# Norms by column sums, true transposes, paired doubling steps and an alternating chain in a PE-bound hybrid decoder step

## The chip, the cores and the metric

One core of a Trainium2 chip runs the whole program. The metric is the device time of one execution in microseconds, as the median of several runs; lower is better. The profile is of one further execution.

## The reference

The program is one inference step of a one-layer decoder with d_model 1024: a prompt of 512 tokens with 16 learned meta tokens in front (528), and 8 sample sequences of 4 tokens, 560 columns in all.

```python
h = rms_norm(x, g_mix); proj = h @ w_in          # all input projections at once
# branch A: GLU -> causal depthwise conv (width 31) -> LayerNorm -> swish -> w_cout
# branch B, 8 heads of 128:
qkv_c = silu(causal_depthwise_conv(qkv, qkv_buf, w_short))   # width 4
q = l2_normalize(heads(q)) * D_HEAD ** -0.5; k = l2_normalize(heads(k)); v = heads(v)
# per chunk (gdn_intra, gdn_inter):
A = tril(beta * (k @ k.T) * decay, -1) + I
value, kcum = solve(A, [v * beta, k * beta * exp(G)])
u = value - kcum @ S
o = q_dec @ S + (q @ k.T * decay) @ u
S = S * exp(g_last) + k_dec.T @ u
o = rms_norm(o, g_head) * silu(z); dn_out = o @ w_dout
mix = sigmoid(gate_c) * conv_out + sigmoid(gate_d) * dn_out
x = x + mix @ w_o
x = x + square(relu(rms_norm(x, g_mlp) @ w_up)) @ w_down      # final rms_norm follows
```

Every matmul has to be of fp32 quality. The states of convolutions and heads come in for the sample sequences and go out for all.

## The kernel before, in words

Activations lie transposed: channels on the 128 partitions, tokens along the free axis. A projection chunk (L605, `gemm`) is 128 output channels: for each of 8 blocks of input channels the weights are split into a high part `wh` and a rest `wl`, the input likewise, and three products are summed, each over two halves of the tokens. That is 48 matmuls of 272 to 280 columns for a chunk. The chunks go in a fixed order: k of all heads first, then GLU pairs mixed with q, v and z of head after head, the gates, then w_dout ("do"), which needs all heads, then the gate of branch A, w_cout, w_o and the MLP (L2054, L2196).

Everything else is threaded between these matmuls by a planner written in Python, the `Weaver`. Each piece of work is a generator that yields (engine, cost, what it depends on). The planner keeps one clock for each engine and at every turn emits the instruction that could start earliest; ties go by priority. The costs are guesses written in the code, as 0.22 for a matmul. Once emitted, each engine runs its own list strictly in order: what the planner misjudged becomes a wait. The planner adds 0.5 us between a result of ACT and a matmul that reads it.

The prompt's delta rule runs in 4 chunks ("quarters", j) of 128 tokens; the last 16 prompt tokens and the 32 sample tokens are a fifth piece of 48. The parts that the change touches:

- `doubling` (L1041): the inverse of the 128 x 128 triangular matrices of all 32 (head, quarter) pairs is built up by blocks. Its last step multiplies 64 x 64 blocks: 32 matmuls at L1100, their results copied to SBUF by ACT and DVE in four lots, 32 matmuls at L1111, four lots copied again.
- `head_prep` (L1380), one head after another: squares of q, v and k turned to token-major. It holds one PSUM bank `b4` for the short piece: `v4` and `k4` are turned by a matmul with the identity (L1403, L1405), k times q is formed (L1407), and the sums of squares of q come token-major from five matmuls that load the squares and stream one column of ones (L1411). Then v (L1444), k (L1453), the product k q (L1461) and its masking on DVE in four pieces (L1465); the first masked piece releases `chain`.
- `chain` (L1473): for each quarter, k S and q S (L1495, L1497), R on DVE (L1501) and a scaled copy on ACT (L1504), the solve (L1510), the copy u (L1512), and two products of u (L1514, L1517) for the new S and the output. All use one PSUM bank `bx`, whose four column ranges have fixed roles. Afterwards the sample sequences: eight products with their states in 32-column tiles (L1538), a zero fill (L1542), the prompt's tail rows (L1544), a copy on ACT (L1546), and two selection matmuls (L1549) that add the samples' rows to what L1542 and L1544 wrote.
- `head_post` (L1631): norm and gate of the head's output, turned back by L1652 and, for the short piece, by a matmul with 48 columns of the identity (L1661).

An fp32 matmul with full operands runs as two passes (x2 in the rows, each with its own weight load); a transpose and the split projection products run as one. `column_sums` (L864) is the form that the norms of x and k use already: ones (or one column of ones) of 32 columns are loaded, the squares are streamed, and the four blocks of tokens go to four groups of 32 output partitions. Its result is turned to token-major by `sums_to_tokens` (L872; L882 a transpose, L885 a small matmul).

## Time and profile before

| | us |
|---|---|
| runs before: median, lowest, highest (3) | 1068.65, 1068.43, 1073.45 |
| the profiled execution's own time | 1068.22 |
| its span | 1066.4 |
| PE busy | 1047.8 (98%) |
| DVE busy | 767.8 (72%) |
| ACT busy | 623.1 (58%) |
| POOL busy | 149.2 (14%) |

The span is the time from the first to the last instruction that the profile has. Busy time is the time in which at least one instruction of the engine was under way; matmuls overlap, so a busy PE can still lose time between them. In the chain of waits every piece begins where the one before ends, so its length is what the program waited for it. "x10" counts passes, not matmuls.

### The profile page before, as it was taken

How to read it: one execution, taken by the hardware profiler on the slowest of the kernel's cores; microseconds unless marked ns; L12 is line 12 of the kernel's file. 1: busy time of each engine (PE TensorE's matmuls, PEld its weight loads, DVE VectorE, ACT ScalarE, POOL GpSimd, SP SyncE). 2: the span in 40 equal slices, each digit the busy share in tenths (PEclk: the TensorE clock that was granted, in tenths of full speed). 3: DMA queues.
4: the chain of work that ended last, by engine and by line, in shares of the span. 5: the costliest groups of instructions: out<-in, count | busy, mean ns of one | idle time of the engine just before them, and what ended most of it. 6: DMA issues, size and time to landing. Idle time of an engine off the chain costs nothing.

```text
span 1066.4 us, 21825 instructions
## 1 busy us (share of the span) xinstructions
PE 1047.8 (98%) x8835; PEld 1025.5 (96%) x8835; DVE 767.8 (72%) x1354; ACT 623.1 (58%) x1285; POOL 149.2 (14%) x173
## 2 busy tenths in 40 slices
PE   8999999999999999999999999999999999999997
PEld 6989999999999999999999999989999999999996
DVE  5888879788889887789953456897458547745754
ACT  5577344668787878775359334677327426723741
POOL 2067211102211221122111000000000000000000
PEclk9999999999999999999999999999999999999999
DMA  6232677466676566678876422753365365346212
GB/s 213 82 90 74 131 173 159 102 141 154 147 174 158 146 141 160 148 178 193 174 168 159 165 98 80 184 143 104 100 183 129 100 159 136 102 118 169 80 61 84
DMA packets 57872, 145.55 MB, mean 136 GB/s; under 512 B 14612, under 2 KB 20140, under 8 KB 57772
## 3 DMA queue, kind: packets, MB, share of 16 engines
q1 hardware_dynamic: 46828, 104.32, 30.5%
q0 software_dynamic: 10944, 39.85, 23.1%
q8 instruction: 69, 1.13, 0.4%
q14 instruction: 31, 0.25, 0.1%
HBM read 135.14 MB, written 9.01 MB: 135 GB/s over the span
## 4 chain that ended last, share of the span: by engine, by line
PE 85%; DVE 7%; DMA 3%; ACT 2%; issue 2%; SPq 0%; POOL 0%; POOLq 0%; DVEq 0%; ACTq 0%
PE pg L605 42%; PE pg L2196 17%; PE bk L2054 15%; DMA pre<-in_sq_dram 1%; DVE V L1209 1%; DVE acc L807 1%; DVE of L807 1%; PE bk L1411 1%; PE bk L1510 1%; PE bk L1514 1%; PE bk L970 1%; PE bk L1517 1%; PE bk L1495 1%; DMA M<-in_xT_dram 1%; PE bk L1497 1%
## 5 line engine op out<-in xcount | busy, mean ns | idle before, releaser
L605 PE MATMUL pg<-R,wh 128*128 128x280 f32 (+2 forms) x1920 | 279.3, 294 | 1.0 <-ACT pre L795 1.0
L605 PEld LDWEIGHTS pg<-R,wh 128*128 128x128 f32 x1920 | 253.6, 189 | 3.9 <-issue 1.5
L1209 DVE SCALAR_TENSOR_TENSOR V<-V,vec,V 128x512 f32<-128x512 f32 x240 | 180.5, 780 | 2.2
L560 ACT ACTIVATE wh<-wraw 128x1024 fp32r<-128x1024 f32 (+1 forms) x89 | 93.4, 1049 | 94.2 <-PE pg L605 79.0
L605 PE MATMUL pg<-R,wl 128*128 128x280 f32 (+2 forms) x960 | 143.9, 294 | 0.0
L605 PEld LDWEIGHTS pg<-R,wl 128*128 128x128 f32 x960 | 128.5, 189 | 1.4 <-issue 1.0
L573 POOL DMA_DIRECT2D wl<-in_w_dram x60 | 52.6, 877 | 343.1 <-ACT wl L571 246.2
L2001 ACT ACTIVATE whm<-RT 128x512 fp32r<-128x512 f32 x73 | 45.6, 626 | 55.3 <-PE pg L2196 40.2
L571 ACT ACTIVATE wl<-wh 128x1024 fp32r<-128x1024 f32 x60 | 63.5, 1058 | 14.8 <-PE pg L605 12.9
L1956 POOL DMA_DIRECT2D RT<-in_wu_dram x16 | 13.9, 866 | 384.1 <-DVE wlm L2004 123.1
L2004 DVE TENSOR_TENSOR wlm<-RT,whm 128x512 fp32r<-128x512 f32 x73 | 50.0, 687 | 16.6 <-issue 8.4
L2054 PE MATMUL bk<-R,whm 128*128 128x272 f32 x340 | 58.3, 288 | 0.7 <-ACT Tt L2095 0.7
L2196 PE MATMUL pg<-RD,whm 128*128 128x272 f32 (+2 forms) x272 | 57.7, 288 | 0.0
L2196 PE MATMUL pg<-K,whm 128*128 128x272 f32 (+2 forms) x272 | 57.5, 288 | 0.0
L605 PE MATMUL pg<-K,wh 128*128 128x272 f32 x256 | 53.0, 288 | 0.2 <-DVE K L1758 0.2
L605 PE MATMUL pg<-RD,wh 128*128 128x272 f32 x256 | 53.1, 289 | 0.0
L2054 PEld LDWEIGHTS bk<-R,whm 128*128 128x128 f32 x340 | 48.7, 188 | 0.9 <-ACT Tt L2095 0.9
L2196 PE MATMUL pg<-RD,M 128*128 128x272 f32 x264 | 46.2, 288 | 0.0
L2054 PE MATMUL bk<-R,M 128*128 128x272 f32 x258 | 45.5, 288 | 0.0
L2001 ACT ACTIVATE whm<-wrawm 128x512 fp32r<-128x512 f32 x43 | 26.8, 623 | 31.6 <-PE pg L2196 29.7
L2212 DVE TENSOR_TENSOR V<-pg,pre 128x544 f32<-128x544 f32 x29 | 21.0, 724 | 32.1 <-PE pg L2196 32.1
L577 DVE TENSOR_TENSOR wl<-wraw,wh 128x1024 fp32r<-128x1024 f32 x28 | 35.1, 1252 | 12.1 <-ACT wh L560 8.0
(485 smaller groups left out, 2453.3 us busy)
## 6 DMA issues: line engine op xcount, KB each, us to landing
wraw<-in_w_dram SPq DMA_DIRECT2D x87, 512.0 KB, 3.6
wl<-in_w_dram POOLq DMA_DIRECT2D x60, 512.0 KB, 5.6
RT<-in_wu_dram SPq DMA_DIRECT2D x24, 512.0 KB, 4.9
RT<-in_wu_dram POOLq DMA_DIRECT2D x16, 512.0 KB, 6.5
wrawm<-in_wn_dram SPq DMA_DIRECT2D x16, 512.0 KB, 3.4
RT<-in_wn_dram SPq DMA_DIRECT2D x16, 512.0 KB, 3.5
M<-in_sd_dram SPq DMA_DIRECT2D x16, 256.0 KB, 3.6
out_osd_dram<-M SPq DMA_DIRECT2D x16, 256.0 KB, 4.0
```

The source lines that it names most:

```text
L560: nc.scalar.activation(wh[:, c[0]:c[1]], w[:, c[0]:c[1]], AF.Copy)
L571: nc.scalar.activation(wl, wh.bitcast(F32), AF.Copy, scale=-1.0)
L573: nc.gpsimd.dma_start(wl, i["w"][n].bitcast(F32R), accum_op=ALU.add)
L577: nc.vector.tensor_tensor(wl, w, wh.bitcast(F32), op=ALU.subtract)
L605: nc.tensor.matmul(pt[:, hf, 0:N], w[idx][:, k, :], x[:, off + hf * N:off + hf * N + N], start=k == 0 and not part and x is hi, stop=k == ...
L807: nc.vector.scalar_tensor_tensor(acc[:, 0:584], pr[:, q:q + 584], vcol(w + q), acc[:, 0:584], op0=ALU.mult, op1=ALU.add)
L1209: nc.vector.scalar_tensor_tensor(cc[:, 0:512], G[r][:, 16 + q:528 + q], vcol(w + q), cc[:, 0:512], op0=ALU.mult, op1=ALU.add)
L2001: nc.scalar.activation(hi, raw, AF.Copy)
L2004: nc.vector.tensor_tensor(lo, raw, hi.bitcast(F32), op=ALU.subtract)
L2054: nc.tensor.matmul(acc[an], w[:, kp, :], x, start=kp == 0 and not part and x is hi and m not in (3, 6, 7), stop=kp == 3 and part == 1, ski ...
L2196: nc.tensor.matmul(out, w[:, k % 4, :], x[:, a], start=n_ == 0 and x is hi, stop=n_ == len(STEPS) - 1)
L2212: nc.vector.tensor_tensor(halves(tmp[:, 0:NPOST]), pt[:, :, 0:NPH], halves(ml["r2"]), op=ALU.mult)
```

## The change

The diff, cut to its core:

```diff
@@ kfin
-            nc.vector.tensor_tensor(st["sk"][:], st["s"][:], st["ed"][:], op=ALU.mult)
@@ doubling
-            for m in range(32):
+            def first(m, cost):
+                tb_[m // 8] = yield op("pe", cost, tn[m // 16], tb)
                 nc.tensor.matmul(B[m // 8][64:128, m % 8, :], KT[0:64, m, 64:128], Tn[0:64, m, :], start=True, stop=True)
+            def second(m, cost):
+                q = m // 8
+                tb_[q] = yield op("pe", cost, t1[q], *tc_[2 * (m // 16):2 * (m // 16) + 2])
+                nc.tensor.matmul(B[q][0:64, m % 8, :], P2[m // 16][64:128, m % 16, :], CTT[64:128, m, 64:128],
                                  start=True, stop=True)
+            for q in (0, 1):
+                for m in range(8 * q, 8 * q + 8):
+                    yield from first(m, 0.116)
+                yield from keep(q)
+            for q in (2, 3):
+                for m in range(8 * q, 8 * q + 8):
+                    yield from first(m, 0.07)
+                    yield from second(m - 16, 0.07)
+                yield from keep(q)
+                yield from done(q - 2)
+            for q in (2, 3):
+                for m in range(8 * q, 8 * q + 8):
+                    yield from second(m, 0.116)
+                yield from done(q)
@@ head_prep
-            nc.tensor.matmul(b4[:96, 0:128], M2["v4"], ident, start=True, stop=True)
-            nc.tensor.matmul(b4[:wk, 128:256], k4, ident, start=True, stop=True)
-            nc.tensor.matmul(b4[:wk, 384:432], k4, kq4[:, hh, :, 1], start=True, stop=True)
-            for j in range(5):
-                w = 128 if j < 4 else 96
-                nc.tensor.matmul(b4[:w, 432 + j:433 + j], sq[:, 128 * j:128 * j + w], ones[:, 0:1], start=True, stop=True)
+            nc.tensor.transpose(b4[:96, 0:128], M2["v4"], ident)
+            if wk > 64:
+                nc.tensor.transpose(b4[:wk, 128:256], k4, ident)
+            else:
+                nc.tensor.matmul(b4[:wk, 128:256], k4, ident, start=True, stop=True)
+            nc.tensor.matmul(b4[:wk, 256:304], k4, kq4[:, hh, :, 1], start=True, stop=True)
+            ts = yield from column_sums(b4[:, 304:480], sq, ones[:, 0:32], t, tb4)
...
-                nc.scalar.activation(kx[r:r + 32], b4[:32, 128:256], AF.Copy, scale=st["sk"][:32, hh, 4:5])
+                nc.scalar.activation(kx[r:r + 32], b4[:32, 128:256], AF.Copy, scale=st["ed"][:32, hh, 4:5])
...
+            nc.scalar.activation(sq[:, 0:128], b4[:, 304:432], AF.Copy)
+            nc.scalar.activation(sq[96:128, 128:176], b4[96:128, 432:480], AF.Copy)
+            nc.tensor.transpose(b4[:, 304:432], sq[:, 0:128], ident)
+            nc.tensor.matmul(b4[0:48, 432:464], sq[96:128, 128:176], ident[96:128, 96:128], start=True, stop=True)
             if hh >= 2:
                 yield wait(("post", hh - 2))
+            nc.vector.tensor_scalar(ssq[:, 0:4], b4[:, 304:432:32], 1e-6, 128.0 * 128.0 * EPS, op0=ALU.add, op1=ALU.mult)
+            nc.vector.tensor_scalar(ssq[:48, 4:5], b4[:48, 432:433], 1e-6, 128.0 * 128.0 * EPS, op0=ALU.add, op1=ALU.mult)
...
-            for j in range(4):
-                nc.vector.scalar_tensor_tensor(at[:, j, :], b[:, 128 * j:128 * j + 128], st["s"][:, hh, j:j + 1],
-                                               Ds[hh][:, j, :], op0=ALU.mult, op1=ALU.mult)
+            nc.vector.tensor_tensor(at, b.rearrange("p (t c) -> p t c", c=128), Ds[hh], op=ALU.mult)
+            W.spawn(chain(hh), -1)
@@ chain
+                ba, bu = (bx[:, 256:384], bx[:, 0:128]) if j % 2 else (bx[:, 0:128], bx[:, 256:384])
-                    t = yield op("pe", 0.22, ts, to)
-                    nc.tensor.matmul(bx[:, 0:128], ks, S, start=True, stop=True)
+                    t = yield op("pe", 0.22, ts)
+                    nc.tensor.matmul(ba, ks, S, start=True, stop=True)
...
-                t = yield op("pe", 0.3, t, t2, tr, tbx)
-                nc.tensor.matmul(bx[:, 256:384], CT["T"][:, 4 * hh + j, :], rr, start=True, stop=True)
-                nc.scalar.activation(u, bx[:, 256:384], AF.Copy)
+                t = yield op("pe", 0.3, t, to, tr, tbx)
+                nc.tensor.matmul(bu, CT["T"][:, 4 * hh + j, :], rr, start=True, stop=True)
+                nc.scalar.activation(u, bu, AF.Copy, scale=st["s"][:, hh, j:j + 1])
...
-            for a in range(2):
-                nc.tensor.matmul(bx[64 * a:64 * a + 32, 256:384], zsel[:, 32:64], ident, start=True, stop=True)
-                nc.tensor.matmul(bx[64 * a + 32:64 * a + 48, 256:384], kq4[:, hh, 32:48, a], S, start=True, stop=True)
             for g in range(2):
                 nc.tensor.matmul(bx[0:96, 256:384], cst[:, C_SL + 96 * g:C_SL + 96 * g + 96], Wt[:, g, :],
-                                 start=False, stop=g == 1, skip_group_check=True)
+                                 start=g == 0, stop=False, skip_group_check=True)
+            for a in range(2):
+                nc.tensor.matmul(bx[64 * a + 32:64 * a + 48, 256:384], kq4[:, hh, 32:48, a], S, start=False,
+                                 stop=a == 1, skip_group_check=True)
...
-            nc.scalar.activation(u[:48], bx[:48, 0:128], AF.Copy)
+            nc.scalar.activation(u[:48], bx[:48, 0:128], AF.Copy, scale=st["s"][:48, hh, 4:5])
@@ head_post
-            nc.tensor.matmul(b4[:, 0:48], ob[:, 4, :], ident[:, 0:48], start=True, stop=True)
+            nc.tensor.transpose(b4[:, 0:128], ob[:, 4, :], ident)
```

In words. The squares of q are summed by `column_sums` into four groups of partitions, copied to SBUF by two ACT instructions, and turned to token-major by a transpose and a small matmul in the same bank; the two DVE instructions that finish the norm come after that, and so do the steps of v and k that follow in `head_prep`. The turns of `v4`, `k4` (but for the last head) and of the output's short piece become transposes. The factor s = beta / |k|^2 no longer scales kd, kx and the masked product but u, in its copy. The masked product is one DVE instruction over all four quarters. In `chain` the column ranges of the output product and of the solve swap from quarter to quarter, so that the first product of a quarter is written where u was read, not where the output is being read. The two zero fills go; the tail rows are added after the selection matmuls. In the last step of `doubling`, half of the two sets of matmuls are issued in turns. Two memsets and a product on DVE go.

## Rows read from the trace of the kernel before

**Rows 1.** The page, part 1: busy us, share of the span, instructions

```profile
PE 1047.8 (98%) x8835; PEld 1025.5 (96%) x8835; DVE 767.8 (72%) x1354; ACT 623.1 (58%) x1285; POOL 149.2 (14%) x173
```

**Rows 2.** Windows, 187 to 492 us: busy us (instructions) by engine, granted clock, DMA

```profile
187.00:492.00 305.00, 302.32 (x2604) 292.90 (x2604) 254.28 (x497) 235.91 (x626) 60.25 (x71) 1.00 0.65 151
```

**Rows 3.** Waits, PE's longest and one of ACT's: us in total, times, longest

```profile
PE bk L1495 <- ACT M L1529: 1.6, 2, 1.0
...
ACT M L1504 <- DVE M L1501: 9.4, 14, 1.3
```

**Rows 4.** Chain of waits from 25 us: start us, us, what (x passes)

```profile
25.36 18.77 PE pg L605 x144
```

**Rows 5.** Chain of waits, first head's preparation

```profile
202.93 2.04 PE pg L605 x16
204.98 0.22 PE bk L1403 x2
...
205.42 0.13 PE bk L1407 x2
205.55 1.02 PE bk L1411 x10
206.57 1.89 PE pg L605 x14
208.46 0.44 PE bk L1444 x4
```

**Rows 6.** Chain of waits, norm of k and its turning back

```profile
96.65 1.33 PE bk L869 x29
97.98 2.52 PE pg L605 x18
100.50 0.11 PE bk L882
100.61 0.20 PE bk L885 x2
100.81 1.24 PE pg L605 x8
```

**Rows 7.** Chain of waits, sample stage of two heads

```profile
403.54 0.36 PE bk L1538 x8
403.90 0.45 PE pg L605 x2
...
471.67 0.36 PE bk L1538 x8
...
472.24 2.97 PE pg L605 x22
475.21 0.44 PE bk L1549 x4
```

**Rows 8.** Chain of waits, doubling; then the line of its third 32x32 product

```profile
189.12 3.87 PE bk L1100 x64
192.99 1.75 PE pg L605 x12
194.74 3.87 PE bk L1111 x64
...
L1084 PE MATMUL bk<-RT,M x64: 191/191/212, 183.8 to 185.8; 32*32 32x32 f32 x64
```

**Rows 9.** Groups of ACT by line, 187 to 492 us: busy us, mean ns | idle

```profile
L571 ACT ACTIVATE wl<-wh 128x1024 fp32r<-128x1024 f32 x33 | 35.0, 1059 | 0.1
...
L1504 ACT ACTIVATE M<-bk,st_eG 128x128 f32<-128x128 f32 x24 | 8.8, 366 | 9.4 <-DVE M L1501 9.4
L1512 ACT ACTIVATE M<-bk 128x128 f32<-128x128 f32 x32 | 8.7, 271 | 4.8 <-PE bk L1510 4.6
```

**Rows 10.** Timeline at the end of the heads: DVE, then PE

```profile
488.94 0.71 DVE L1677 TENSOR_TENSOR K<-zs,RD 128x544 fp32r<-128x544 f32 x1
...
495.51 0.41 PE L605 MATMUL pg<-RD,wh 128*128 128x272 f32 x2
```

More of the change, by code (lines that the diff above doesn't have):

```diff
@@ L1314, in m2 @@
                 m2_["kd"] = [cut(640).rearrange("p (t c) -> p t c", c=128) for _ in range(2)]
-                aa = [cut(608) for _ in range(2)]
+                aa = [cut(560) for _ in range(2)]
                 m2_["aa"] = aa
@@ L1428, in head_prep @@
             tx = yield op("act", 0.25, t4)
-            nc.scalar.activation(kd[32:48, 4, :], b4[32:48, 128:256], AF.Copy, scale=st["sk"][32:48, hh, 4:5])
+            nc.scalar.activation(kd[32:48, 4, :], b4[32:48, 128:256], AF.Copy, scale=st["ed"][32:48, hh, 4:5])
             if hh >= 2:
@@ L1434, in head_prep @@
                 tx = yield op("act", 0.25, t4)
-                nc.scalar.activation(kx[r:r + 32], b4[:32, 128:256], AF.Copy, scale=st["sk"][:32, hh, 4:5])
-            t = yield op("dve", 0.2, tx)
-            nc.vector.scalar_tensor_tensor(kx[64:96], b4[:32, 128:256], st["sk"][:32, hh, 4:5], kx[0:32].bitcast(F32),
+                nc.scalar.activation(kx[r:r + 32], b4[:32, 128:256], AF.Copy, scale=st["ed"][:32, hh, 4:5])
+            tk = yield op("dve", 0.2, tx)
+            nc.vector.scalar_tensor_tensor(kx[64:96], b4[:32, 128:256], st["ed"][:32, hh, 4:5], kx[0:32].bitcast(F32),
                                            op0=ALU.mult, op1=ALU.subtract)
-            E(("kx", hh)).set(t)
-            put_bank(kb4, t)
+            E(("kx", hh)).set(tk)
+            yield op("act", act_c(128), ts)
+            nc.scalar.activation(sq[:, 0:128], b4[:, 304:432], AF.Copy)
+            t = yield op("act", act_c(48), ts)
+            nc.scalar.activation(sq[96:128, 128:176], b4[96:128, 432:480], AF.Copy)
+            yield op("pe", 0.12, t)
+            nc.tensor.transpose(b4[:, 304:432], sq[:, 0:128], ident)
+            t = yield op("pe", 0.06, t)
+            nc.tensor.matmul(b4[0:48, 432:464], sq[96:128, 128:176], ident[96:128, 96:128], start=True, stop=True)
+            if hh >= 2:
+                yield wait(("post", hh - 2))
+            t1 = yield op("dve", 0.1, t)
+            nc.vector.tensor_scalar(ssq[:, 0:4], b4[:, 304:432:32], 1e-6, 128.0 * 128.0 * EPS, op0=ALU.add, op1=ALU.mult)
+            t1 = yield op("dve", 0.1, t)
+            nc.vector.tensor_scalar(ssq[:48, 4:5], b4[:48, 432:433], 1e-6, 128.0 * 128.0 * EPS, op0=ALU.add, op1=ALU.mult)
+            E(("ssq", hh)).set(t1)
+            put_bank(kb4, max(t1, tk))
             b, kb, tb = yield from get_bank()
@@ L1455, in head_prep @@
                 tx = yield op("act", 0.25, t)
-                nc.scalar.activation(kd[:, j, :], b[:, 128 * j:128 * j + 128], AF.Copy, scale=st["sk"][:, hh, j:j + 1])
+                nc.scalar.activation(kd[:, j, :], b[:, 128 * j:128 * j + 128], AF.Copy, scale=st["ed"][:, hh, j:j + 1])
             put_bank(kb, tx)
@@ L1462, in head_prep @@
                                  q[:, 128 * j:128 * j + 128], start=True, stop=True)
-            for j in range(4):
-                t1 = yield op("dve", 0.263, t)
-                nc.vector.scalar_tensor_tensor(at[:, j, :], b[:, 128 * j:128 * j + 128], st["s"][:, hh, j:j + 1],
-                                               Ds[hh][:, j, :], op0=ALU.mult, op1=ALU.mult)
-                E(("at", hh, j)).set(t1)
-                if j == 0:
-                    E(("ready", hh)).set(max(t1, tx))
-                    W.spawn(chain(hh), -1)
+            t1 = yield op("dve", dve_c(512), t)
+            nc.vector.tensor_tensor(at, b.rearrange("p (t c) -> p t c", c=128), Ds[hh], op=ALU.mult)
+            E(("at", hh)).set(t1)
             put_bank(kb, t1)
+            E(("ready", hh)).set(max(t1, tx))
+            W.spawn(chain(hh), -1)
         def chain(hh):
@@ L1508, in chain @@
                     t, t2 = tr, 0.0
-                t = yield op("pe", 0.3, t, t2, tr, tbx)
-                nc.tensor.matmul(bx[:, 256:384], CT["T"][:, 4 * hh + j, :], rr, start=True, stop=True)
+                t = yield op("pe", 0.3, t, to, tr, tbx)
+                nc.tensor.matmul(bu, CT["T"][:, 4 * hh + j, :], rr, start=True, stop=True)
                 tu = yield op("act", 0.17, t)
-                nc.scalar.activation(u, bx[:, 256:384], AF.Copy)
+                nc.scalar.activation(u, bu, AF.Copy, scale=st["s"][:, hh, j:j + 1])
                 t = yield op("pe", 0.22, tu)
                 nc.tensor.matmul(bx[:, 384:512], kd[:, j, :], u, start=True, stop=True)
-                ta = yield wait(("at", hh, j))
+                ta = yield wait(("at", hh))
                 to = yield op("pe", 0.22, tu, ta)
-                nc.tensor.matmul(bx[:, 0:128], at[:, j, :], u, start=True, stop=True)
+                nc.tensor.matmul(ba, at[:, j, :], u, start=True, stop=True)
                 Sn = Sb[j % 2]
```

56 lines of the change are left out of this document (17 added, 39 removed).

## The prediction

> **What bounds the kernel now.** I read the page's busy times first. TensorE (PE) is busy for 98% of the span, so it decides unless another engine starves it [rows 1]. Next comes the stage in which the change works, read by windows: from the doubling to the last head's output, 187 to 492 us, PE is busy 302 of 305 us, VectorE (DVE) 254 and ScalarE (ACT) 236, and the granted clock is 1.00, the 2.4 GHz level [rows 2]. The waits come third: the longest entry for PE in the whole trace is 1.6 us [rows 3]. So in this stage the heads' small matmuls are threaded between those of the projections (L605), and an instruction taken from PE shortens the stage by what it took there, whatever it did to latency; time taken from DVE or ACT is worth nothing unless PE waits for it. The busy share can't price these instructions, since matmuls overlap in it. The chain of waits can: where it runs along PE, its pieces join end to end, and a piece is what PE needed to get past that work. There a projection matmul takes 0.130 us at 280 columns (18.77 / 144) and 0.1275 at 274 (2.04 / 16) [rows 4, 5].
>
> **Head preparation, before.** Row by row: v4 0.22, k4 likewise 0.22, kq 0.13, the five column-of-ones sums 1.02, and the 14 projection matmuls behind them take 1.89 where 14 x 0.1275 is 1.78, so 0.11 more: 1.70 us for a head [rows 5]. A transpose is one pass instead of two: four take 0.44, 0.11 each [rows 5].
>
> **Head preparation, after.** The new sums use a form that the trace has in the norm of k: 32 loaded columns, four such tiles side by side. Sixteen of them (32 passes, of which the chain names 29) take 1.33, and the 18 projection matmuls behind take 2.52 instead of 2.34, so 1.51 in all [rows 6]. That isn't four times the price of four. The sample stage shows why: eight passes of 32-column tiles take 0.36, and the two projection matmuls after them 0.45 instead of the 0.255 of two at 274 columns, 0.56 in all; the next eight passes without a projection between take only 0.57 - 0.36 = 0.21 (472.24 - 471.67 is 0.57) [rows 7]. So going from whole-width matmuls into tiles and back costs 0.35 each time, and the work itself little. Four sums alone are then (1.51 - 0.35) / 4 + 0.35 = 0.64. Turning them back is the pair L882 and L885: 0.11 + 0.20, and eight projection matmuls at 1.24 instead of 1.04, 0.51 [rows 6]; it stands apart from the sums, because two ACT copies come between. After: v4 and k4 0.11 each, kq 0.13, sums 0.64, turning back 0.51, together 1.50, or 0.20 less for a head. Eight heads give -1.5, since the last one keeps its k4 matmul.
>
> The Trainium skill weighs in on both sides here. "TensorE: Matmul & The Clock Gate", Part 3 (measured speedup vs the span model), gives a set of tiles one matmul's duration and about 4 ns for each further tile, by which the sums would cost only what they stream; "TensorEngine Tiling (Array Packing)", Tiling Modes (key properties), says that a change of the tiling mode drains the engine. The 0.35 us above agrees with the second, and the first alone leads to rival A.
>
> **Output transpose (L1661).** Now two passes that load 128 columns; the sums of that form take 1.02 / 5 = 0.20 though they stream one column [rows 5]. As a transpose it takes 0.11: -0.09, for eight heads -0.7.
>
> **Sample queries in the chain.** The zero fill (L1542) goes, and the two matmuls of the lead segment (L1544) move behind the selection matmuls (L1549, 96 loaded columns, 0.44 for four passes [rows 7]). Before, the four ran in the tile mode that L1538 had opened already and cost the 0.21 above. After, the two that are left still stream for two passes, but between whole-width work, so they open the mode for themselves: 0.21 + 0.35 = 0.56. That is +0.35 for a head, +2.8 for eight. I take it whole, because a group that streams just as long costs 0.56 in the rows; the bounds are -1.7 (nothing but the four old ones goes) and +2.8.
>
> **Doubling.** The two sets of 32 matmuls of 64 x 64 take 3.87 each, and 12 projection matmuls behind the first take 1.75 instead of 1.56: 4.06, twice 8.1 [rows 8]. One matmul is 3.87 / 32 = 0.12. The edit pairs 16 of each set on opposite quarters of the array. That such tiles do run beside each other is seen one step earlier: its loop issues three matmuls of 32 x 32 to three places of the array in each of 32 steps, two passes each, and the third line's 64 passes all lie within 183.8 to 185.8 us [rows 8], 0.03 us for three passes. What is paired then falls from 32 x 0.12 = 3.8 to between 1.9 and 3.8; I take 2.2, near the first. The price is that the work falls from two blocks into about six, as each quarter's copy to SBUF lets projection matmuls in: 4 x 0.35 = 1.4 more. Sum -1.6 + 1.4 = -0.2; the ends are -1.9 (still two blocks) and +1.4 (six blocks, no overlap).
>
> **Alternating quarters and s in u.** L1495 no longer overwrites what L1529 has still to read. PE's wait there is 1.6 us in two places [rows 3]. But the quarter's solve now waits for that same read, half a step later, and the copy of u gains a scale operand: L1512 without takes 0.27 us, L1504 with one 0.37 [rows 9]. I take -1.0, bounds -1.6 and 0. Four masked products in one go, no product sk, fewer memsets: these are DVE's and POOL's, which have 51 and 245 us free in the stage [rows 2]; nothing.
>
> **Waits that are added.** PE's turning back waits for two ACT copies, and behind it on PE's queue stand the projections. ACT then has about 0.7 us more for a head (two copies, each bounded above by the 0.37 of L1504) and 69 us free [rows 2, 9]. With the longest wait at 1.6 us [rows 3], PE's many other hand-overs from ACT cost next to nothing, as the planner leaves 0.5 us for each. I take +0.3; the ends are 0 and rival C. The bank of the sums is held longer, and v, k and kq of a head start later by the round trip, some 2 us. Where that could show is the end: the last head's low part is ready at 488.94 + 0.71 = 489.65, and the projections of "do" reach its high part at 495.51 [rows 10]. Cover of about 5.9 us is left, so nothing; without it, each us of delay beyond would be one us of span.
>
> **Sum.** -1.5 - 0.7 + 2.8 - 0.2 - 1.0 + 0.3 = -0.3 us. The profiled span of 1066.4 becomes 1066.1; that execution's own time was 1068.2, 1.8 more, and the median of the runs shown lies 0.4 above it. So 1068.3 by the median: no change. Below, a change under 0.5% (5.3 us) counts as none, which is about what a measurement of this kernel can tell from no change.
>
> **Rivals.** A, the tiles cost only what they stream: sums 0.29, turning back 0.31, so 0.95 instead of 1.70 for a head, -6.0; output -0.7; sample queries 0; doubling -1.9; waits -1.0. Sum -9.6, 1059 us. For it speaks that passes inside one mode are that cheap; against it the slow projection matmuls behind every such block [rows 6 to 8]. The span model of the Trainium skill, named above, would give this one.
> B, the alternation does not do what it says: L1495 still waits, because the waits go by the whole bank. For it: ACT's L1504 is released by DVE's L1501 14 times, 9.4 us, though they read different columns [rows 3]. Against: PE waited for L1529 only, which did read the columns overwritten. Time: +1.0, 1069.3.
> C, slower: ACT's copy of the sums falls behind a weight copy (L571, 1.06 us [rows 9]) that the planner had put after it, and PE, in order, stands still at the transpose. It decides once the copy is over 0.5 us late; if every head is hit by a whole weight copy, 8 x 1.06 = +8.5, 1077 us; by half of one, about 1072. For it: ACT is held by late transfers now and then. Against: the same order of engines at L1510 to L1514, 32 times over, left no row near the top of PE's waits.
>
> **Chances.** Forecast 0.58, A 0.10, B 0.18, C 0.14. The likeliest case alone spans its own unknowns, doubling -1.9 to +1.4 and alternation -0.6 to +1.0 around the values taken, and the order that the planner finds anew: 1065 to 1071. For eight in ten I widen it towards A and C to 1063.5 to 1072. Faster by over 0.5% (under 1063.3): most of A and an edge of the forecast, 0.11. Slower by over 0.5% (over 1074): the upper half of C, 0.07. Same: 0.82.
>
> **What would show it.** In the chain of waits after: column sums of a head as 8 passes with some 0.3 to 0.4 us, and projection matmuls behind them 0.2 late; the same behind L1544's new place, as a piece of its own; transposes of 0.11 for v4, k4 and the output; doubling in six pieces, two of them with both lines side by side in about 1.1 us each. PE's wait at the first product of a quarter for L1529 gone. Wrong would be: no lateness behind the tile groups (A), a row of PE waiting for ACT at the new transpose (C), or PE idle ahead of "do".

## The result and the profile after

The changed kernel takes 1075.4 us (median of 6 runs, 1075.17 to 1076.7) and the kernel before 1068.66 in the runs beside it: the ratio is 1.0057, 95% interval 1.0043 to 1.0071. It is slower, and above the forecast range. The profiled span is 1073.4 us (before 1066.4), that execution's time 1075.27.

The page's busy times, to be set beside [rows 1], and the heads' stage by windows, to be set beside [rows 2] (columns as there):

```profile
PE 1053.2 (98%) x8788; PEld 1019.3 (95%) x8788; DVE 759.7 (71%) x1329; ACT 631.8 (59%) x1301; POOL 149.5 (14%) x171
```

```profile
187.00:494.50 307.50, 304.97 (x2544) 284.36 (x2544) 249.16 (x476) 242.40 (x640) 61.02 (x69) 1.00 0.64 150
```

PE is as full as before: it sits idle 2.5 us of this window and 2.7 us of the one before, and the granted clock is 1.00 in both. So waits and the clock do not make the stage longer. Both windows begin at 187 us, where the changed kernel is 1.4 us further in its work; between the same two projection matmuls it has 48 instructions fewer on PE and takes 3.9 us more. So fewer instructions cost more time each. The busy share alone would have hidden that.

To place the loss I lined up the projections' matmuls (L605, the same sequence in both traces), 48 at a time, and took at each the start after less the start before. The changed kernel begins 1.4 us early (x arrives earlier in that execution; it varies from run to run). From the end of the norm of k to the end of the first projection chunk of "do" it loses 3.9 us, which I call the stage's step below. Then nothing for 15 groups, 4.5 us in the next two, and nothing to the end. So two separate losses, 3.9 in the heads and 4.5 behind them, less the 1.4 at the start: 7.0, the difference of the spans.

**Behind the heads.** PE's waits in the whole trace, against [rows 3] (us in total, times, longest), and the chain of waits from 578 us:

```profile
PE pg L605 <- DMA wl<-in_w_dram: 2.7, 1, 2.7
...
PE bk L1450 <- ACT M L1448: 0.9, 1, 0.9
```

```profile
578.89 1.28 ACT L1731
...
580.18 2.85 ACT K L1731 x5
...
584.94 1.06 ACT wl L571
...
586.28 8.96 DMA wl<-in_w_dram
...
595.28 4.81 PE pg L605 x24
```

The longest wait is a new one, PE waiting for low weights. Reading the chain backwards: the transfer took 8.96 us, was issued after ACT's L571, and that stood behind ACT's table load (1.28) and five of the gate's activations (2.85). In the kernel before, the chain of this stretch is one row of PE alone, L571 ran ahead of the table load, and the last of these transfers was issued 8 us ahead of the loads of x (chain of waits, then timelines of ACT, POOL and SyncE):

```profile
574.88 25.19 PE pg L605 x201
...
580.61 1.05 ACT L571 ACTIVATE wl<-wh 128x1024 fp32r<-128x1024 f32 x1
...
582.40 1.28 ACT L1713 ACT_TABLE_LOAD   x1
...
581.96 0.86 POOL L573 DMA_DIRECT2D wl<-in_w_dram  x1 [4.96 <-ACT wl L571]
...
590.21 4.10 SPq L1769 DMA_DIRECT2D V<-in_xT_dram  x8
```

Now SyncE issues the loads of x while the transfer runs:

```profile
585.84 3.44 SPq L1787 DMA_DIRECT2D V<-in_xT_dram  x6
```

The wait itself is 2.7 of the 4.5 us. Behind it the granted clock fell, part of the time to the 1.2 GHz level (windows), and the 24 matmuls at 595.28 took 4.81 us, where 24 at the 25.19 / 201 of the kernel before take 3.0. That is the other 1.8 us.

```profile
595.28:598.70 3.42, 3.42 (x18) 3.42 (x19) 0.10 (x1) 0.15 (x1) 0.00 (x0) 0.64 0.77 307
```

**In the heads.** First head's preparation and a tail in the chain of waits, against [rows 5] and [rows 7]:

```profile
204.69 0.11 PE bk L1416
204.80 0.11 PE bk L1419
204.91 0.13 PE bk L1423 x2
205.04 0.44 PE bk L869 x8
205.48 3.01 PE pg L605 x22
208.48 0.11 PE bk L1450
208.59 0.20 PE bk L1452 x2
208.79 1.22 PE pg L605 x8
```

```profile
246.27 0.44 PE bk L1563 x4
246.71 0.25 PE pg L605 x2
246.96 0.32 PE bk L1567 x2
247.28 0.45 PE pg L605 x2
247.73 0.32 PE bk L1567 x2
248.05 0.42 PE bk L1529 x2
```

The preparation is the forecast to the digit: 0.11, 0.11, 0.13, the sums 0.44 and 0.20 of lateness in the 22 projection matmuls behind (3.01 less 22 x 0.1275), the turning back 0.31 and again 0.20 (1.22 less 8 x 0.1275). The tail is not. The forecast had the two tail matmuls side by side, one entry into the tile mode for a head. The trace shows a projection pair between them: each is a block of its own, 0.32 for itself and 0.20 on what follows it, 0.52 twice. Over the whole stage L1567 enters the mode 15 times and not 8, and the sample products (L1557) 15 times instead of 12. All of PE's list has 71 entries into a tile mode where the one before has 34; these and the counts below are along the list that PE gets, and the traces give the same to within one.

The doubling, against [rows 8] (pieces of the pairs are short, since the two lines alternate):

```profile
187.05 1.07 PE bk L1102 x16
188.12 0.97 PE pg L605 x6
...
190.16 0.46 PE pg L605 x2
190.62 0.20 PE bk L1102
190.81 0.01 PE bk L1107
190.82 0.05 PE bk L1102
...
195.49 1.07 PE bk L1107 x16
```

It comes in six blocks, as forecast. Inside a pair L1107 adds 0.01 to each step of L1102: a block of 16 + 16 passes costs 1.28 with its entry, one of 16 passes 1.27. The pairs overlap wholly, and the doubling costs 7.6 instead of 8.1.

The cover at the end, against [rows 10], by the timeline of DVE and of PE:

```profile
494.53 0.73 DVE L1695 TENSOR_TENSOR K<-zs,RD 128x544 fp32r<-128x544 f32 x1
```

```profile
498.02 0.41 PE L605 MATMUL pg<-RD,wh 128*128 128x272 f32 x2
```

The last head's low part is done at 495.26, and PE wants its high part at 498.02: 2.8 us of the 5.9 are left. The heads end later by more than PE does.

### The profile page after: what moved, and what is told of

It is laid out like the page before. It is cut to its first block, busy times and chain, and to the rows that moved or that the text cites. A ratio compares the mean times of both kernels' runs of the same rounds, so it can differ in the third digit from the quotient of the medians.

```text
span 1073.4 us, 21720 instructions
## 1 busy us (share of the span) xinstructions
PE 1053.2 (98%) x8788; PEld 1019.3 (95%) x8788; DVE 759.7 (71%) x1329; ACT 631.8 (59%) x1301; POOL 149.5 (14%) x171
## 3 DMA queue, kind: packets, MB, share of 16 engines
q0 software_dynamic: 10944, 39.85, 22.9%
## 4 chain that ended last, share of the span: by engine, by line
PE 87%; DVE 5%; ACT 3%; DMA 3%; issue 2%; SPq 0%; POOL 0%; POOLq 0%; DVEq 0%; ACTq 0%
PE pg L605 44%; PE pg L2214 17%; PE bk L2072 15%; DVE acc L807 1%; DMA wl<-in_w_dram 1%; PE bk L1529 1%; PE bk L1481 1%; PE bk L970 1%; PE bk L869 1%; PE bk L1533 1%; DVE V L1223 1%; DMA M<-in_sd_dram 1%; PE bk L1536 1%; PE bk L1557 1%; PE bk L1514 0%
## 5 line engine op out<-in xcount | busy, mean ns | idle before, releaser
L605 PE MATMUL pg<-R,wh 128*128 128x280 f32 (+2 forms) x1920 | 281.7, 295 | 1.0 <-ACT pre L795 1.0
L605 PEld LDWEIGHTS pg<-R,wh 128*128 128x128 f32 x1920 | 254.0, 189 | 7.8 <-issue 4.8
L1223 DVE SCALAR_TENSOR_TENSOR V<-V,vec,V 128x512 f32<-128x512 f32 x240 | 177.1, 769 | 2.0
L605 PE MATMUL pg<-R,wl 128*128 128x280 f32 (+2 forms) x960 | 147.9, 298 | 2.7 <-DMA wl<-in_w_dram 2.7
L605 PEld LDWEIGHTS pg<-R,wl 128*128 128x128 f32 x960 | 129.6, 190 | 5.5 <-DMA wl<-in_w_dram 3.0
L571 ACT ACTIVATE wl<-wh 128x1024 fp32r<-128x1024 f32 x60 | 63.5, 1058 | 17.7 <-PE pg L605 16.3
L605 PE MATMUL pg<-K,wh 128*128 128x272 f32 x256 | 52.9, 288 | 0.2 <-DVE K L1776 0.2
L605 PE MATMUL pg<-RD,wh 128*128 128x272 f32 x256 | 53.1, 289 | 0.0
```

The lines of the kernel that those rows point to most:

```text
L571: nc.scalar.activation(wl, wh.bitcast(F32), AF.Copy, scale=-1.0)
L605: nc.tensor.matmul(pt[:, hf, 0:N], w[idx][:, k, :], x[:, off + hf * N:off + hf * N + N], start=k == 0 and not part and x is hi, stop=k == ...
L1223: nc.vector.scalar_tensor_tensor(cc[:, 0:512], G[r][:, 16 + q:528 + q], vcol(w + q), cc[:, 0:512], op0=ALU.mult, op1=ALU.add)
```

## The experiments

Theory at the start: the 4.5 us are the transfer beside the loads of x, and the 3.9 us are entries into the tile mode, above all at L1567. Rival: they are waits for other engines. Each ratio is against the kernel before in the same session (its medians 1068.7 to 1071.2), with the 95% interval. "Step" is that of the heads' stage, from the profile: one execution, up to 4.3 us off its kernel's median (f3_alt 3.6 below it, n0_before 3.9 above). "Idle" is the time in that stage in which PE has nothing under way, by windows; it is 2.7 us in the kernel before and 2.5 in the changed one.

### The transfer beside the loads of x

**e1_xlate**: the loads of x are planned after the last chunk that needs the transfer.

```
             yield wait("ln")
+            yield wait(("mm", A1 - 1))
```

> The changed kernel, with the eight loads of x (L1787 of the changed kernel) let go only after the low part of projection chunk 71, the last whose low weights come by an accumulating transfer. Theory: of the 7 us that the changed kernel lost in its profile, 4.5 are lost at chunk 71/72 because these loads now run beside that transfer (8.96 us instead of about 5.5). Then the wait of PE for that transfer goes, everything up to chunk 71 stays as it is, and the time is 4.5 us lower: about 1070.9. Rival (the transfer is late because ACT's copy ahead of it comes late, behind a table load): the wait stays, 1075.4.

**e4_a71**: the transfer gives way in one chunk, whose low weights DVE makes.

```
-        A0, A1 = 12, 72
+        A0, A1 = 12, 71
```

> The changed kernel, with the low weights of chunk 71 made by DVE from the raw weights, as those of 72 and later are, instead of by the accumulating transfer. Theory (the transfer of chunk 71 runs beside the loads of x): PE's wait there goes or moves to chunk 70 with under 1 us; about 1071 to 1072. Rival (the loads of x disturb any transfer, or ACT's order is what is late): a wait of 2 us or more stays at chunk 70 to 72.

Measured: e1_xlate 1.0029 (1.0016 to 1.0042), e4_a71 1.0029 (1.0018 to 1.0040). The loss at that place falls from 4.5 us to 0.7 and to 0, and half of the slowdown goes with it. The transfer in e1_xlate, by the chain of waits:

```profile
588.33 6.63 DMA wl<-in_w_dram
```

So this loss is shown, twice: it belongs to the order that the planner chose, not to any instruction of the change. In e1_xlate ACT still comes late and only the loads of x are gone from beside the transfer for most of its time, so the lateness is worth at most 0.7 us. The step of the heads stays (5.0 and 4.8).

### Entries into the tile mode in the changed kernel

**e2_tailpair**: the second tail matmul no longer depends on the first, so that the two can stand together.

```
             for a in range(2):
-                t2 = yield op("pe", 0.1, t2, ts)
+                t2 = yield op("pe", 0.1, ts, *((t2,) if a == 0 else ()))
```

> The changed kernel, with the dependence of the second tail-row matmul (L1567) on the first taken out of the planner's list, so that the two stand side by side on PE's list. Theory: the changed kernel enters the tiles 15 times for these 16 matmuls instead of 8 as forecast, because the planner puts 0.2 us between two dependent matmuls and a projection pair slips in; each single one costs 0.52 us, a pair 0.56. With 7 fewer entries (15 to 8 by groups of blocks) the stage from chunk 21 to 'do' is 3 to 4 us shorter. Rival (the entries are hidden and the stage lost its time elsewhere, in waits of the solve): under 1 us. Either way the wait at chunk 71 may move with the order.

**e3_tailold**: zero fill and tail rows as before the change, behind the sample products.

```
+            for a in range(2):
+                yield op("pe", 0.03, ts, to)
+                nc.tensor.matmul(bx[64 * a:64 * a + 32, 256:384], zsel[:, 32:64], ident, start=True, stop=True)
...
-            for a in range(2):
-                t2 = yield op("pe", 0.1, t2, ts)
```

> The changed kernel, with the sample queries' part as before: zero fill and tail rows right behind the eight sample products, ahead of the copy and the selection matmuls. Theory: the tail rows then run in a mode that is open already, 0.21 us a head instead of about 1.0; the stage from chunk 21 to 'do' is some 6 us shorter, 2 us shorter than in the kernel before. Rival (entries hidden): no change of the stage.

Measured: e2_tailpair 1.0051 (1.0034 to 1.0067), step 4.2 with 64 entries instead of 71; e3_tailold 1.0194 (1.0168 to 1.0220), step 18.5 with 57. Both went against the theory. PE's waits had grown instead: for L1523 at the solve 3.2 us in the first, and in the second some 14 us for ACT, POOL and DVE, 2.7 of them at the first projection of "do". Against the changed kernel, e2_tailpair has 3.2 us more of idle time and a step that is 0.3 longer; PE's own work has thus become 2.9 us shorter, where 7 entries at 0.35 are 2.5. So the theory failed on the time, and the price held. Two things had to be told apart from here: the price of an entry, and what a new order of the heads costs.

### The parts alone, on the kernel before

Each takes one part of the change's diff and leaves the rest.

**f1_trans_dbl**: the one-pass transposes and the paired doubling.

```
+                    yield from first(m, 0.07)
+                    yield from second(m - 16, 0.07)
...
-            nc.tensor.matmul(b4[:96, 0:128], M2["v4"], ident, start=True, stop=True)
...
+            nc.tensor.transpose(b4[:96, 0:128], M2["v4"], ident)
```

> The kernel before with two parts of the change alone: the one-pass transposes (v4 and k4 of a head, output of a head) and the paired doubling. By the unit costs 15 transposes for 15 two-pass matmuls give 15 x 0.11 = -1.65 us, the output 8 x 0.09 = -0.7, the doubling -0.2 (forecast) to -0.5 (the profile after): -2.6 to -2.9 us by the stage from the doubling to the first projection chunk of 'do', about 1066 by the time where the kernel before is 1068.7. Rival: the stage is not bound by the PE instructions but by the chain of each head, so taking passes off PE moves nothing (0 us).

**f2_tailmove**: the tail rows behind the selection, without the zero fill.

```
+            for a in range(2):
+                t2 = yield op("pe", 0.1, t2, ts)
+                nc.tensor.matmul(bx[64 * a + 32:64 * a + 48, 256:384], kq4[:, hh, 32:48, a], S, start=False,
...
```

> The kernel before with one part alone: the two matmuls of the lead segment moved behind the selection matmuls, the zero fill gone. The list of PE has them going into the tile mode 16 times (two a head, a projection pair between them). Theory (each opening costs 0.35 us, an opening with one two-pass matmul about 0.52): 16 x 0.52 less 8 x 0.21 for the four old ones = +6.6 us in the stage. Rival, the forecast's own term (one opening a head): +2.8 us. Second rival (openings are hidden, the loss of the stage is waits): about -1.7 to 0 us.

**f3_alt**: the alternating quarters.

```
+                ba, bu = (bx[:, 256:384], bx[:, 0:128]) if j % 2 else (bx[:, 0:128], bx[:, 256:384])
...
-                    t = yield op("pe", 0.22, ts, to)
+                    t = yield op("pe", 0.22, ts)
```

> The kernel before with the alternating quarters alone (no factor s in u, tail rows in their old place). Theory: PE's waits for the reader of the output quarter only move to the solve (L1529's counterpart), so the stage moves by 0 us, plus up to +0.7 for two more openings of the sample products. Rival, the forecast's term: -1.0 us, with no PE wait above 0.5 us left for DVE or ACT at the solve.

**f5_norms**: the column sums of q and their turning back.

```
-                nc.tensor.matmul(b4[:w, 432 + j:433 + j], sq[:, 128 * j:128 * j + w], ones[:, 0:1], start=True, stop=True)
...
+            ts = yield from column_sums(b4[:, 304:480], sq, ones[:, 0:32], t, tb4)
```

> The kernel before with the column sums of q alone (v4 and k4 still by two-pass matmuls, factor s where it was). By the unit costs 0.64 for the sums and 0.51 for turning them back replace 1.02 and 0.11 of lateness, 1.15 for 1.13: 0 us for eight heads, plus 0 to 0.5 us for waits at the new transpose. Rival (the waits for ACT's copies are what makes the changed kernel slower): +3 us or more in the stage, with PE waiting for ACT at the turning back.

| alone | ratio | step, us | expected |
|---|---|---|---|
| f1_trans_dbl | 0.9957 (0.9941 to 0.9974) | -3.1 | -2.6 to -2.9 |
| f2_tailmove | 1.0052 (1.0034 to 1.0069) | +6.4 | +6.6, forecast +2.8 |
| f3_alt | 1.0053 (1.0037 to 1.0069) | +4.4 | 0 to 0.7, forecast -1.0 |
| f5_norms | 1.0043 (1.0027 to 1.0060) | +5.0 | 0 to 0.5 |

The second is the decisive one for the tail: the chain of waits shows the same two blocks, and PE's idle time grew by only 0.6 us (1.6 at L1495, as before), so 16 entries at 0.52 less the old 1.7 is what was lost.

```profile
243.20 0.32 PE bk L1548 x2
243.52 0.46 PE pg L605 x2
243.98 0.32 PE bk L1548 x2
244.30 0.98 PE pg L605 x6
```

The third and fourth I had wrong. f3_alt by PE's waits:

```profile
PE bk L1497 <- ACT M L1531: 3.9, 3, 2.2
```

L1497 there writes quarter 256:384 and L1531 reads quarter 0:128, yet PE waits for it, three times. So the wait goes by more than the quarter, as rival B had it: by the bank, it seems (a dependency through the tile M, which both lines also touch, was not told apart). And because the planner was told that nothing has to be waited for, it moved L1497 up: 14 projection matmuls ahead of it (1.8 us) in the first head, where the kernel before has 20 (2.6 us). ACT's copy is not done by then, and PE, in order, stands. Idle time grew by 3.4 us, and two more entries at the sample products are 0.7. f5_norms by PE's waits:

```profile
PE pg L605 <- ACT RD L1680: 2.2, 1, 2.2
PE bk L1435 <- ACT M L1433: 2.0, 3, 1.2
```

Here both covers of the forecast fail: the turning back waits for the copies, and the first projection of "do" waits for the last head. Idle time grew by 3.1 us, and behind the second wait the granted clock fell for a stretch (0.995 over the stage). An estimate of what that costs is the length of the stage times what the clock lacks of 1.00, 1.7 us here; behind the heads of the changed kernel the same product (clock 0.64 and 0.85 over 595.28 to 602 us) gives 1.7 where 1.8 was measured. Together 4.8 of the 5.0 are accounted for, and the sums themselves cost the 0 that their prices gave.

### Telling the planner, and fewer entries

**g1_alt_told**: f3_alt, with the dependencies of the kernel before given to the planner.

```
-                    t = yield op("pe", 0.22, ts)
+                    t = yield op("pe", 0.22, ts, to)
...
-                t = yield op("pe", 0.3, t, to, tr, tbx)
+                t = yield op("pe", 0.3, t, t2, to, tr, tbx)
```

> The kernel before with the alternating quarters, as in f3_alt, but the planner is told that a quarter's first products wait for the reader of the other quarter and its solve for the copy of q S (the dependencies that the kernel before gave it). PE's order is then the one of the kernel before. Theory (the program waits by the whole bank, and f3_alt lost 4.4 us because the planner was told otherwise): stage within 0.5 us of the kernel before, and PE still waits some 1.6 us for the ACT copy of the first output though it reads another quarter. Rival (waits go by quarter, f3_alt lost in another way): that wait is gone and the stage is 1 to 1.6 us shorter.

**g4_told**: the same edit in e4_a71.

> The changed kernel with the low weights of one chunk fewer by the accumulating transfer (as e4_a71) and the planner told of both waits (as g1_alt_told). Openings 72 instead of 71. Theory: PE's wait of 0.7 us for the copy of q S at the solve goes, the stage changes by -1 to 0 us against e4_a71, about 1072.5. Rival (untold waits cost as much here as the 4.4 us of f3_alt): -4 us, about 1069.

**g2_tailold_told**: the same edit in e3_tailold, and A1 = 71.

> The changed kernel with the tail rows in their old place (as e3_tailold), the planner told of both waits (as g1_alt_told), and the low weights of one chunk fewer by the accumulating transfer (as e4_a71). 15 openings fewer than in the changed kernel. Theory (the 22 us that e3_tailold lost are waits that the planner was not told of): about 6 us less than e4_a71, near 1067. Rival (the longer hold of the bank and the round trip of the column sums make the heads late, as f5_norms showed at the end of the stage): the first projection of 'do' still waits for the last head and the time stays at 1075 to 1090.

**g3_s0both**: f1_trans_dbl, and the sample products wait for both halves of the state.

```
+            tS0 = max((yield wait(("S0", hh, 0))), (yield wait(("S0", hh, 1))))
             for g in range(2):
-                tS0 = yield wait(("S0", hh, g))
```

> f1_trans_dbl (one-pass transposes and paired doubling alone), and the sample products of a head wait for both halves of its state, so that their 8 matmuls are one block: PE's list has 8 openings at that line instead of 13. By 0.35 us an opening: -1.75 us against f1_trans_dbl, some 1065. Rival: the wait for the second half of the state holds PE or the heads, and the time is that of f1_trans_dbl or 1 to 2 us above.

Measured: g1_alt_told 1.0001 (0.9991 to 1.0010), step 0.75, with PE's order that of the kernel before and the wait unchanged:

```profile
PE bk L1497 <- ACT M L1531: 1.8, 2, 1.2
```

This settles the alternation: in the old order it removes no wait, and most of the 4.4 us of f3_alt is the planner's, misled. g3_s0both, 13 entries at that line to 8: 0.9955 (0.9941 to 0.9969), 1065.1 us, step -5.4. Against f1_trans_dbl the step gives 2.3 where 1.75 was expected (a wait for the state went as well); by the times, 1066.6 and 1065.1, the two are not apart. It is faster than the kernel before and than the changed one. g2_tailold_told 1.0169 (1.0142 to 1.0196), step 11.5, and g4_told 1.0196 (1.0178 to 1.0214), step 25.1, came out far from what was expected: telling the planner more did not bring the heads of the changed kernel back in time. So the untold waits are not what made e3_tailold slow. And g4_told differs from e4_a71, whose step is 4.8, in what the planner is told alone: a new order by itself cost 20 us in the stage, 17 by the times.

### Entries taken out, and the heads' second limit

**h1_lead**: e4_a71, and the two tail matmuls as one of full width, from a zeroed buffer that holds both sets of 16 columns. 56 entries.

```
+            nc.vector.tensor_copy(lp.rearrange("p (a c) -> p a c", c=64)[:, :, 32:48],
+                                  kq4[:, hh, 32:48, :].rearrange("p t a -> p a t"))
...
+            nc.tensor.matmul(bx[:, 256:384], M2["lp"][p], S, start=True, stop=False, skip_group_check=True)
```

> The changed kernel with one chunk's low weights fewer by the accumulating transfer (as e4_a71), and the lead segment's two 16-column products as one product of full width (its two sets of columns copied into a zeroed 128-column buffer by DVE). PE's list then has 56 openings instead of 71. Theory (the tail rows are mis-sized in the forecast: 15 openings of about 0.52 us in the changed kernel): 15 x 0.52 goes, 8 x 0.22 comes, -6.0 us against e4_a71 in the stage, some 1067. Rival (the stage of the changed kernel is lost to waits that any new order brings, as in e2_tailpair and g4_told): no gain or a loss against e4_a71, with PE waiting several us for DMA, POOL or ACT.

**h2_lead_s0**: h1_lead with the edit of g3_s0both. 50 entries.

> h1_lead, and the sample products of a head as one block of 8 matmuls (as g3_s0both): 50 openings on PE's list, 8 instead of 15 at that line. Theory: 7 x 0.35 = 2.5 us less than h1_lead in the stage, some 1064.5. Rival: as for h1_lead, waits in place of the openings, no gain.

Measured: 1.0145 (1.0120 to 1.0169) and 1.0284 (1.0260 to 1.0309), steps 14.7 and 27.8. The rival held: fewer entries, more time, with 12.9 and 22.9 us of idle time. The chain of waits of h2_lead_s0 shows one thing that the heads then wait for:

```profile
491.96 0.70 DVE M L1644
492.68 5.90 DMA out_osd_dram<-M
498.60 5.83 DMA M<-in_sd_dram
504.56 0.53 PE bk L1563 x8
```

A head's states lie in one buffer. Its update (L1636 to L1644) must be stored and the next head's states loaded before that head's sample products (L1563) can start, and in the kernels so far they start on the second half of a state 3 to 14 us, mostly 4 to 7, after its load's issue (the first head aside): there is hardly any slack. On average the heads' sample products are 32.7 us apart in the kernel before, 31.9 in the changed one, and 36.6 in h2_lead_s0. The theory: when the heads fall behind, the projections run out, and PE has nothing left to fill its waits with. To test it I left the update out: no scaling, no sum; the states are stored as loaded, so the buffer comes free early. This edit in four kernels:

```
+                W.spawn(keep_s0(hh, g, t), 0)
...
-                    tx = yield op("act", 0.25, tu)
-                    nc.scalar.activation(S0[:, 4 * q4 + b, :], S0[:, 4 * q4 + b, :], AF.Copy,
...
```

**n0_before**, on the kernel before:

> The kernel before, with the update of the samples' states left out (no scaling by ACT, no sum by DVE; the states are stored as they were loaded), so that the one state buffer is free for the next head as soon as the sample products and the store have read it. Its PE list has the same products and 29 openings instead of 34. Theory (the kernel before is bound by PE's list, the cycle through the state buffer is only close behind): 5 x 0.35 = 1.75 us and some of the 2.5 us of waits go, -2 to -4 us in the stage. Rival (the cycle through the state buffer already sets the stage before): -10 us or more.

**n1_a71**, on e4_a71:

> The changed kernel as in e4_a71, with the update of the samples' states left out as in n0_before: 65 openings. Against n0_before it shows the change without the cycle through the state buffer. Theory (openings): 36 more openings at 0.35 = +12.6 us, less some 8 us of passes saved: +4 to +5 us on n0_before in the stage. Rival (the change's cost is latency in the heads' cycle): within 1 us of n0_before, or faster.

**n2_lead_s0**, on h2_lead_s0:

> h2_lead_s0 with the update of the samples' states left out as in n0_before: 50 openings. Theory (openings cost what they cost, and h2_lead_s0 was slow because the heads' cycle through the state buffer fell behind): the tail rows' 16 x 0.52 go and 8 x 0.22 come, 6.6 us less than n1_a71 in the stage, and no wait of PE for the state's load. Rival (other waits than the state's cycle hold these orders back): no better than n1_a71, with PE waiting for ACT, DVE or POOL.

**n3_g3**, on g3_s0both:

> g3_s0both with the update of the samples' states left out as in n0_before: 34 openings. Theory: transposes -2.4, doubling -0.5, so some 3 us less than n0_before in the stage. Rival (g3_s0both owes its gain to a lucky order): equal to n0_before.

| without the update | ratio | time, us | step, us | idle, more than before | lower clock, estimate as for f5_norms | rest |
|---|---|---|---|---|---|---|
| n0_before | 1.0084 (1.0061 to 1.0107) | 1077.9 | +7.9 | 6.2 | 3.4 | -1.7 |
| n1_a71 | 1.0109 (1.0093 to 1.0124) | 1081.0 | +9.5 | 4.0 | 1.7 | +3.8 |
| n2_lead_s0 | 1.0042 (1.0028 to 1.0057) | 1074.1 | +4.3 | 2.9 | 3.4 | -2.0 |
| n3_g3 | 1.0006 (0.9994 to 1.0019) | 1070.5 | -1.0 | 3.5 | 0 | -4.5 |

n2_lead_s0 is 26 us faster than h2_lead_s0 with the same 50 entries, as the theory has it, and PE no longer waits for the state's load. What that owes to the buffer alone is not shown: the edit also takes some 20 us of work from ACT in the stage. Against n1_a71, which has 65 entries, its step is 5.2 us shorter where 6.6 was expected. What is left is

```profile
PE bk L1520 <- ACT M L1554: 4.1, 4, 3.3
```

By their times n0_before and n3_g3 do not fit: less work made the kernel before 8 us slower in the stage where 2 to 4 less was expected, with PE waiting 8 us for ACT: 4.0 at L1495, 2.0 at L1514 and 2.0 at L1510. The chain of waits of n0_before shows that the edit itself brought the longest of these:

```profile
213.22 7.38 DMA M<-in_sd_dram
...
220.62 0.33 SPq L1601
...
221.00 2.56 DMA pre<-in_sq_dram
...
225.62 0.49 PE bk L1495 x2
```

SyncE issues in order. The new store of the state (L1601) waits there for the state's load, and behind it stands the load of a convolution's state, which the kernel before issued at 216.77 and this one at 221.00; ACT needs it before it comes to the copy that PE waits for. The same store stands ahead of the longest wait of each of the four (3.1, 2.7, 3.3 and 2.6 us), and in the first three the granted clock fell at that wait.

So the last columns take idle time and the lower clock out of the step; the rest is PE's own work. It goes by the prices to about 1 us: n0_before -1.7, where five entries less are -1.75; n1_a71 5.5 above it (4 to 5 expected), n2_lead_s0 5.8 below n1_a71 (6.6), n3_g3 2.8 below n0_before (3). Reckoned so, the other runs come within some 2 us of their prices, but for g4_told (3.5 below). The prices add up for PE's own work; the waits that an order brings are not to be had from their sum.

## Why the prediction was wrong

**What bounds the kernel** held for both kernels compared: PE is full in the stage and the clock granted is 1.00. It missed how little slack the heads' cycle through the state buffer has. That doesn't explain the changed kernel's own loss, but it is part of why mending it failed.

**Head preparation and output** were sized right: each price came out as forecast, and f1_trans_dbl gave the transposes and the doubling together -3.1 where the prices made -2.6 to -2.9. That agreement is in part luck, since its idle time grew by 1.4 us and PE's own work fell by 4.6.

**Sample queries**, the first step that failed: "they open the mode for themselves: 0.21 + 0.35 = 0.56. That is +0.35 for a head, +2.8 for eight." The price was right (0.52), the count was not. The second tail matmul was planned after the first, and PE's list puts a projection pair between two dependent products. 15 entries x 0.52 less the old 8 x 0.21 is +6.1; alone it measured +6.4. Above that, the sample products are now planned before the second half of the state is there, three entries more, +1.0. The bound of +2.8 called the upper end was none. Rival A is refuted: the projection matmuls behind every group of tiles come 0.2 us late. The Trainium skill, "TensorEngine Tiling (Array Packing)", Tiling Modes (key properties), says that a change of the tiling mode drains the engine. The trace agrees again, at 0.35 us for in and out.

**Doubling**: -0.5 instead of -0.2, since the pairs overlap wholly.

**Alternating quarters**, the second: forecast -1.0 because L1495 would wait no longer; it waits still in g1_alt_told, since the waits go by more than the quarter. That run shows that much of rival B, given 0.18; that the bank is what they go by is likely and not shown, and B's 1069.3 us was wrong. In the changed kernel the new order puts the wait at the solve (L1529 for L1523, 0.7 us) in place of the 1.6 at L1495, so the size came out near the forecast, by luck. Alone the edit costs 4.4 us through the planner.

**Added waits**: PE's 0.9 us at L1450 is three times the +0.3 forecast and far from rival C's 8.5. These 0.9 more and the alternation's 0.9 less cancel, and all of PE's idle time in the stage stays as it was (2.5 us for 2.7). But this and the cover at the end hold in the changed kernel only; in f5_norms both fail.

With these sizes the sum for the stage is -1.5 - 0.7 + 6.1 + 1.0 - 0.5 - 0.9 + 0.9 = +4.4 where the trace shows +3.9.

**Nothing in the sum stood for the third failure**: that a change within the heads reorders work 90 us behind them. ACT's gate moved ahead of a weight copy, and an accumulating transfer came to lie beside the loads of x. It cost 4.5 us in the profile (2.7 of waiting, 1.8 at the lower clock behind it) and about 3 by the ratios of e1_xlate and e4_a71 (1.0057 to 1.0029). The prediction's range named the planner's new order as an unknown, and gave it no price.

What stays open: why the planner's orders in e3_tailold, g2_tailold_told, g4_told, h1_lead and h2_lead_s0 are so much worse. Their idle time is 9 to 20 us above that of the kernel before and their granted clock 0.97 to 0.99 over the stage, which is most of each step. But no single cause stands behind their longest waits: in h1_lead and g4_told it is a state's load, in e3_tailold and g2_tailold_told a table load and other work of ACT ahead of a copy, and at the end of four of them DVE's convolution (L1223) ahead of the last head. That the state buffer is the cause in h2_lead_s0 is made likely by n2_lead_s0, for the others it was only argued. A second state buffer was not tried.

## What to carry to other kernels

Count entries into a tile mode in the order that PE will really have, not by the groups in the source: a small tile product that depends on another, or lies between full-width work, pays 0.35 us each time. Before telling a planner that a wait is gone, see in the built program or in a trace that it is: otherwise the order is tightened against a wait that still comes. Where work is threaded between two resources that are both nearly full, try each part alone, take idle time and the granted clock out before holding a price against the time, and look behind the stage changed for what the new order has moved. An edit that leaves work out can put something new in the way: look at its chain of waits before drawing on its time.

## What the runs showed of the hardware

Tiles of 64 x 64 on opposite quarters of the array run wholly side by side: 16 + 16 passes cost 1.28 us and 16 alone 1.27. The same 512 KB accumulating transfer took 8.96 us beside the loads of x and 6.63 when these came later; its median is 5.5 in the changed kernel. And a wait of PE can cost twice: the 2.7 us for low weights in the changed kernel brought 1.8 more. In g4_told, by windows of 10 us, PE stood 2.0 us for a state's load from 424 us on, and the granted clock fell from the 2.4 GHz level to the 1.2 GHz level for part of both stretches:

```profile
420.00:430.00 10.00, 7.75 (x52) 6.17 (x50) 3.36 (x10) 9.88 (x27) 0.88 (x1) 0.82 0.76 189
430.00:440.00 10.00, 8.51 (x52) 7.39 (x51) 7.67 (x15) 5.76 (x14) 0.00 (x0) 0.67 0.17 52
```

Not every such wait does: the 2.2 us in f3_alt left the clock at 1.00.
